# Down projection of a hybrid decoder block: a plain part of six chunks, then two-by-two Strassen products in 26 staggered visits

## Chip, cores and metric

One core of a Trainium2 chip runs the whole kernel in one launch. The metric is device microseconds from the first to the last instruction of the execution; less is better. All tensors are float32. TensorE (PE) multiplies in a reduced float32 form, so each product of two float32 matrices is made of three: high part by high part, high by low, low by high, where `hi` is the operand rounded by ScalarE (ACT) and `lo` the remainder taken by VectorE (DVE).

## The reference, cut to what matters

```python
x = x + merged @ w_o                                   # x: 512 tokens x 2048
h = rmsnorm(x, g_ffn)
u = causal_dwconv(h @ w_up, ffn_conv_w, ffn_conv_b)    # 3 taps, 2 x 5632 channels
ug, uv = split(u, 2)
x = x + (silu(ug) * uv) @ w_down                       # 5632 -> 2048: the down projection
h = rmsnorm(x, g_ple)
x = x + sigmoid(h @ w_ple_gate) * (p @ w_ple_proj)
out = rmsnorm(x, g_final)
```

Ahead of these lines stands the mixer: attention and a convolution branch, merged by gates.

## The kernel before

Activations lie transposed, 128 channels on the partitions and 512 tokens in a row; such a tile (`A()`, one of 75 slots of the pool `slots`) is the moving operand. The weight is the stationary operand, 128x128 per matmul.

`build` makes a list of groups, and `run` goes through their chunks in order. For each chunk it issues the loads of the next six chunks at most (`loads`, on SP's queue, `wraw` has 7 buffers), cuts the weights two or three chunks ahead into `whi` and `wlo` (`prep`, `cut`, L272 on ACT and L273 on DVE, four buffers each), issues the matmuls, evicts, and calls `pump`, which steps each background generator (`add_bg`). A scheduler then orders each engine's instructions; each engine works through its own list in order.

Three kinds of work follow one another behind the mixer:

- **Up projection**, 44 `Pair` groups, one per 128 hidden channels of each half. Each is a two-by-two Strassen product: seven products (`ORDER`), each of 8 weight blocks. A product's weight is one of seven sums of four weight quarters; two of the sums are begun in HBM during the mixer (`sums`, L933: SP copies one quarter, POOL's DMA queue adds another), the others are made by adding a quarter to `wraw` by a POOL DMA after the cut (L310). `pair_step` issues per block one matmul of 512 columns (hi weight by the operand's hi and lo halves) and one of 256 (lo weight by hi). The hidden tiles go to HBM (`hid`).
- **Down projection**, `Group`s over w_down: the 44 chunks of 128 hidden channels are split into `PARTS` of 12, 12, 12 and 8; each part fetches its hidden tiles from HBM and splits them (`fetch`, `split`), and goes through all 16 output tiles in four groups of four. Per chunk and output tile there are three matmuls of 512 columns (`products`, L417), so 44 x 16 x 3 = 2112. After each group `ev_down` (L960) adds the four PSUM tiles to the residual `x1`, which stands in SBUF.
- **Gate**, four groups over w_ple_gate, whose operand `h2` is `x1` split with the norm's weight (`split_x1`, `begin_gate`), while the norm's statistics (`stats("rb3")`, L185) run beside the first group. The last group is done twice, for tokens 0 to 255 and 256 to 511 (`TOK_A`, `again`), so its matmuls have 256 columns.

Of the kernel before, what the change touches and what calls it, by code (L numbers as in the profile page):

```python
# [1 line left out]

# [15 lines left out]
P = 128  # L18
# [41 lines left out]
class Group:  # L60


    def __init__(self, w, rhs, evict, tok=False, before=None, ns=ALL, keep=None):
        self.ns = ns
        self.w, self.rhs, self.evict, self.tok, self.before = w, rhs, evict, tok, before
        self.n = w.shape[0]
        self.nm = w.shape[3] // P
        self.keep = keep


class Pair:
# [9 lines left out]
    def __init__(self, src, rhs, evict, before=None, beside=()):  # L81
        self.src, self.rhs, self.evict, self.before, self.beside = src, rhs, evict, before, iter(beside)
        self.kh = src[1].shape[1]
        self.raw, self.cut, self.ps, self.c = {}, {}, {}, {}


class Kernel:
# [18 lines left out]
    def X(self):  # L106
        return self.aux.tile([P, S], F32, tag="x", name="x")

# [8 lines left out]

    def move(self, out, in_):

        self.nc.gpsimd.dma_start(out=out, in_=in_)  # L120
# [135 lines left out]
    def run(self, groups):  # L256
        nc = self.nc
        chunks = []
        for n, g in enumerate(groups):
# [3 lines left out]
            if not isinstance(groups[n - 1], Pair):  # L263
                chunks.append((g, 5))
            after = groups[n + 1] if isinstance(groups[n + 1], Pair) else None
# [9 lines left out]
        def dma(i, kks=(slice(0, 2),)):  # L275
            if i < len(chunks):
                g, c = chunks[i]
                if isinstance(g, Pair):
# [19 lines left out]
        def prep(i, kks=(slice(0, 2),)):  # L298
# [3 lines left out]
            if isinstance(g, Pair):  # L302
                hi = self.whi.tile([P, g.kh, P], F32R, tag="w", name="whi")
                lo = self.wlo.tile([P, g.kh, P], F32R, tag="w", name="wlo")
                raw = g.raw[{6: 5, 3: 5}.get(c, c)]
                cut(hi, lo, raw)
                g.cut[c] = hi, lo

# [17 lines left out]

        loadx = self.start(dma, prep)
        begun.update(range(3))
        cuts = 1
        for i, (g, c) in enumerate(chunks):  # L330
# [8 lines left out]
            if g.before and c == (5 if isinstance(g, Pair) else 0):  # L339
                g.before()  # L340
            if isinstance(g, Pair):
                self.pair_step(g, c)
                for _ in range(2):
                    next(g.beside, None)
                self.pump()
                continue
# [20 lines left out]
            if c == g.n - 1:  # L367
                g.evict(g.ps)
            self.pump()
# [12 lines left out]
    def pair_step(self, g, c):  # L382
# [21 lines left out]
        if p == 4:  # L404
            g.evict(g.c[1], g.c[6], g.c[4], g.c[5])

# [237 lines left out]
    def build(self):  # L644
# [224 lines left out]
        def fold(c, eng):  # L869
            eng.tensor_tensor(c[:, LEFT], c[:, LEFT], c[:, RIGHT], op=ALU.add)  # L870

# [33 lines left out]
        F0 = [sum(PARTS[:i]) for i in range(len(PARTS))]  # L905
        hs = {}

        def fetch(pi):
            raw = {}
            for f in range(F0[pi], F0[pi] + PARTS[pi] + 2):  # L910
                if f < F0[pi] + PARTS[pi]:
                    raw[f] = self.A()
                    self.move(out=raw[f], in_=hid[f])
                if f - 2 >= F0[pi]:
                    hs[f - 2] = self.split(raw.pop(f - 2))
                yield


        srcs = []
        for j in range(KF):  # L920
            w = t["w_up"][j]
            s1, s3 = (self.dram.tile([P, KD // 2 + 1, P], F32, tag=f"s{n}_{j}", name=f"s{n}_{j}")[:, :KD // 2] for n in (1, 3))
            srcs.append({1: w[0], 2: w[1], 4: w[3], 5: s1, 7: s3})

# [11 lines left out]
        builders = {0: fetch(0)}  # L936
        for j in range(KF):
            groups.append(Pair(srcs[j], lambda p, k: T2[p][k], ev_up(j), before=first_up if j == 0 else None,
                               beside=builders[0] if j == KF - 1 else ()))

        def ready(pi, mg):
            def f():
                if mg == 0:
                    if pi == 0:
                        self.finish_chains()
                    for _ in builders[pi]:
                        pass
                if pi == 0:
                    for m in range(4 * mg, 4 * mg + 4):
                        self.x1[m] = self.A()  # L950
                        self.load(out=self.x1[m], in_=x1d[m])
                if mg == 1 and pi + 1 < len(PARTS):
                    builders[pi + 1] = self.add_bg(fetch(pi + 1))
            return f

        def ev_down(mg):
            def f(ps):
                for m in range(4):
                    z = self.x1[4 * mg + m]
                    nc.vector.tensor_tensor(z, ps[m], z, op=ALU.add)  # L960
            return f

        for pi, n in enumerate(PARTS):
            for mg in range(4):
                groups.append(Group(t["w_down"][mg][F0[pi] // 2:(F0[pi] + n) // 2], lambda k, pi=pi: hs[F0[pi] + k],
                                    ev_down(mg), before=ready(pi, mg)))


        h2, pj = {}, {}

        def split_x1():
            for k in range(KD):
                h2[k] = self.split(self.x1[k], self.col(C_GPLE + k))
                self.nacc = self.square_add(self.x1[k], self.nacc)
                if k % 2:
                    yield
            yield from stats("rb3")()

        def begin_gate():
            self.g_split = self.add_bg(split_x1())  # L980
            next(self.g_split)
            next(self.g_split)

        def load_pj(mg):
            def f():
                if mg == 0:
                    begin_gate()
# [51 lines left out]
        for mg in range(4):  # L1039
            groups.append(Group(t["w_gate"][mg], lambda k: h2[k], ev_gate2(4 * mg, TOK_A if mg == 3 else ALL),  # L1040
# [72 lines left out]
```

## Time and profile before

| | us |
|---|---|
| three runs: median (lowest to highest) | 2762.07 (2758.61 to 2774.99) |
| the profiled execution | 2775.36 |
| its span in the trace | 2773.6 |
| PE busy in it | 2749.3 |
| DVE busy, ACT busy | 1738.3, 1149.1 |

The profiled execution lies 13.3 us above the median of the three runs. Busy time of PE is a modelled time: matmuls are pipelined, and a matmul of 512 columns is listed with 387 ns where the next one starts after some 227 ns. How fast PE goes is therefore read from counts in a stretch of time, and where it waits from its idle time.

### The profile page before, as it was taken

How to read it: one execution, taken by the hardware profiler on the slowest of the kernel's cores; microseconds unless marked ns; L12 is line 12 of the kernel's file. 1: busy time of each engine (PE TensorE's matmuls, PEld its weight loads, DVE VectorE, ACT ScalarE, POOL GpSimd, SP SyncE). 2: the span in 40 equal slices, each digit the busy share in tenths (PEclk: the TensorE clock that was granted, in tenths of full speed). 3: DMA queues.
4: the chain of work that ended last, by engine and by line, in shares of the span. 5: the costliest groups of instructions: out<-in, count | busy, mean ns of one | idle time of the engine just before them, and what ended most of it. 6: DMA issues, size and time to landing. Idle time of an engine off the chain costs nothing.

```text
span 2773.6 us, 34953 instructions
## 1 busy us (share of the span) xinstructions
PE 2749.3 (99%) x13528; PEld 2316.6 (84%) x13528; DVE 1738.3 (63%) x2554; ACT 1149.1 (41%) x1647; POOL 231.3 (8%) x320
## 2 busy tenths in 40 slices
PE   9999999999999999999999999999999999999997
PEld 7888888888888888888888888888888888888787
DVE  5465588658745454478787878787876433335436
ACT  5354452222123333356555555555554322113333
POOL 0010010000000000021111111111111000000000
PEclk9999999999999999999999999999999999999999
DMA  8574756767666674467777777777777433223322
GB/s 278 162 227 134 231 153 182 197 197 194 191 192 186 194 226 146 148 189 199 202 198 202 198 201 198 202 198 201 199 208 277 145 113 103 99 94 112 99 95 95
DMA packets 145303, 489.85 MB, mean 177 GB/s; under 512 B 17136, under 2 KB 21232, under 8 KB 145136
## 3 DMA queue, kind: packets, MB, share of 16 engines
q1 hardware_dynamic: 110048, 363.86, 38.7%
q0 software_dynamic: 34944, 123.75, 22.2%
q8 instruction: 106, 1.74, 0.2%
q14 instruction: 61, 0.50, 0.1%
q10 hardware_dynamic: 144, 0.01, 0.0%
HBM read 457.14 MB, written 116.39 MB: 207 GB/s over the span
## 4 chain that ended last, share of the span: by engine, by line
PE 97%; DVE 1%; issue 1%; ACT 0%; DMA 0%; POOL 0%; POOLq 0%; DVEq 0%; ACTq 0%
PE m L417 65%; PE m L393 20%; PE m L394 10%; PE x L553 1%; PE x L526 0%; PE x L527 0%; PE x L544 0%; DVE wlo L273 0%; DMA a<-hid 0%; DVE o L1033 0%; DVE a L165 0%; PE x L185 0%; DMA gm<-g_mix 0%; PE x L569 0%; POOL sm L217 0%
## 5 line engine op out<-in xcount | busy, mean ns | idle before, releaser
L417 PE MATMUL m<-a,whi 128*128 128x512 f32 (+1 forms) x5056 | 1542.5, 387 | 2.7 <-DVE a L1018 1.4
L273 DVE TENSOR_TENSOR wlo<-wraw,whi 128x1024 fp32r<-128x1024 f32 (+1 forms) x637 | 777.7, 1222 | 784.9 <-ACT whi L272 755.9
L272 ACT ACTIVATE whi<-wraw 128x1024 fp32r<-128x1024 f32 (+1 forms) x637 | 673.1, 1058 | 1360.4 <-PE m L417 899.6
L417 PEld LDWEIGHTS m<-a,whi 128*128 128x128 f32 x5056 | 942.8, 188 | 193.8 <-DVE a L1018 1.7
L417 PE MATMUL m<-a,wlo 128*128 128x512 f32 (+1 forms) x2528 | 976.1, 387 | 0.0
L393 PE MATMUL m<-a,whi 128*128 128x512 f32 x2464 | 871.1, 399 | 3.0 <-ACT a L397 2.0
L394 PE MATMUL m<-a,wlo 128*128 128x256 f32 x2464 | 692.0, 281 | 0.0
L393 PEld LDWEIGHTS m<-a,whi 128*128 128x128 f32 x2464 | 463.0, 188 | 119.3 <-ACT a L397 2.7
L417 PEld LDWEIGHTS m<-a,wlo 128*128 128x128 f32 x2528 | 474.4, 188 | 96.3 <-DVE wlo L273 0.3
L394 PEld LDWEIGHTS m<-a,wlo 128*128 128x128 f32 x2464 | 465.4, 189 | 0.2
L610 DVE SCALAR_TENSOR_TENSOR a<-a,par 128x485 f32<-128x485 f32 (+19 forms) x240 | 172.4, 733 | 6.1 <-ACT a L607 1.6
L933 POOL DMA_DIRECT2D s<-w_up x88 | 72.4, 826 | 827.8 <-DMA s<-w_up 827.8
L890 DVE SCALAR_TENSOR_TENSOR a<-a,par 128x511 f32<-128x511 f32 (+1 forms) x176 | 131.4, 747 | 1.9 <-ACT a L888 0.3
L310 POOL DMA_DIRECT2D wraw<-w_up x88 | 75.1, 854 | 343.2 <-DVE a L883 247.2
L397 ACT ACTIVATE a<-m 128x512 f32<-128x512 f32 x176 | 101.8, 578 | 0.0
L888 ACT ACTIVATE a<-a,par 128x512 f32<-128x512 f32 x88 | 71.1, 808 | 38.7 <-DVE a L885 38.7
L417 PE MATMUL m<-whi,a 128*128 128x512 f32 x256 | 81.7, 394 | 0.4 <-ACT whi L272 0.4
L150 ACT ACTIVATE a<-a 128x512 fp32r<-128x512 f32 x88 | 53.6, 624 | 58.1 <-DVE a L228 23.0
L151 DVE TENSOR_TENSOR a<-a 128x512 fp32r<-128x512 f32 x88 | 59.8, 688 | 17.3 <-ACT a L150 16.8
L217 POOL TENSOR_TENSOR sm<-sm,mhalf 128x4 f32<-128x4 f32 (+1 forms) x14 | 15.7, 1123 | 547.9 <-DVE sm L216 547.9
L120 POOL DMA_DIRECT2D hid<-a x44 | 25.4, 577 | 429.8 <-DVE a L895 429.8
L885 DVE TENSOR_TENSOR a<-a 128x512 f32<-128x512 f32 x88 | 60.2, 684 | 0.2
(136 smaller groups left out, 1348.0 us busy)
## 6 DMA issues: line engine op xcount, KB each, us to landing
wraw<-w_in SPq DMA_DIRECT2D x143, 512.0 KB, 4.2
wraw<-w_up SPq DMA_DIRECT2D x132, 512.0 KB, 3.7
s<-w_up SPq DMA_DIRECT2D x88, 512.0 KB, 5.9
s<-w_up POOLq DMA_DIRECT2D x88, 512.0 KB, 6.9
wraw<-s SPq DMA_DIRECT2D x88, 512.0 KB, 4.6
wraw<-w_up POOLq DMA_DIRECT2D x88, 512.0 KB, 5.5
wraw<-w_down SPq DMA_DIRECT2D x88, 512.0 KB, 3.5
wraw<-w_o SPq DMA_DIRECT2D x32, 512.0 KB, 3.6
```

The source lines that it names most:

```text
L272: nc.scalar.activation(hi, w, AF.Copy)
L273: nc.vector.tensor_tensor(lo, w, hi.bitcast(F32), op=ALU.subtract)
L310: nc.gpsimd.dma_start(out=raw, in_=g.src[{5: 1, 6: 2}[c]], accum_op=ALU.add)
L393: nc.tensor.matmul(ps, lhsT=hi[:, k], rhs=t, start=new and k == 0, stop=False, skip_group_check=True)
L394: nc.tensor.matmul(ps[:, LEFT], lhsT=lo[:, k], rhs=t[:, LEFT], start=False, stop=k == g.kh - 1, skip_group_check=True)
L397: nc.scalar.activation(x, ps, AF.Copy)
L417: nc.tensor.matmul(out, lhsT=l, rhs=r, start=first and n == 0, stop=last and n == 2)
L610: nc.vector.scalar_tensor_tensor(y[:, s:], u[:, :S - s], self.col(w + k), y[:, s:], op0=ALU.mult, op1=ALU.add)
L885: nc.vector.tensor_tensor(u, u, rb, op=ALU.mult)
L888: nc.scalar.activation(y, u, AF.Identity, scale=self.col(w + 2), bias=self.col(C_FB + ch))
L890: nc.vector.scalar_tensor_tensor(y[:, s:], u[:, :S - s], self.col(w + 2 - s), y[:, s:], op0=ALU.mult, op1=ALU.add)
L933: nc.gpsimd.dma_start(out=src[n], in_=w[h], accum_op=ALU.add)
```

## The change

The 5632 hidden channels are split: the first `F0` = 6 chunks stay plain, the other 38 make `KP` = 19 pairs. For these the down projection is a two-by-two Strassen product: two output tiles (`o` and its partner, 8 such pairs of tiles), two halves of the hidden channels of a pair, two halves of the tokens (`LEFT`, `RIGHT`, 256 each).

- `feed` fetches two hidden tiles of a pair and makes seven operand tiles of them (`operands`, as in the up projection: 4 sums and 7 hi/lo cuts of 256 columns). They are kept in `T3`, and as 19 x 7 don't fit into 75 slots, the outputs are visited in four rounds, staggered by one pair each: `VISITS` lists output, first and last pair.
- A visit with `kh` pairs has seven steps (`NARROW`). `visit_step` issues for each pair three matmuls of 256 columns into half a PSUM bank. The weight sums: one ("s") is made in HBM by `sums` behind those of the up projection (L993), two are added by DVE (L327, L329), one by a POOL DMA into `wraw` after the cut for product 6 (L333).
- Partial results, of the plain part too, are added to the residual in HBM by POOL DMAs (`ev_plain`, L1046, and L1077). At an output's last visit `x1` is loaded and summed on DVE (L1066), split into `h2`, and squared for the norm's statistics.
- The gate takes its operand in the order in which the outputs end (`GATE_K`).

```diff
-PARTS = [12, 12, 12, 8]
+F0 = 6
+KP = (KF - F0) // 2
+ENDS = [[2, 3, 4, 5, 6, 7, 8, 8], list(range(9, 17)), [min(n, KP) for n in range(17, 25)], [KP] * 2]
+NARROW = [1, 5, 6, 2, 7, 3, 4]
...
             if isinstance(g, Pair):
                 hi = self.whi.tile([P, g.kh, P], F32R, tag="w", name="whi")
                 lo = self.wlo.tile([P, g.kh, P], F32R, tag="w", name="wlo")
+                if not g.wide:
+                    a = g.raw
+                    if c == 6:
+                        nc.vector.tensor_tensor(a["s"], a["s"], a[0], op=ALU.add)
+                    elif c == 7:
+                        nc.vector.tensor_tensor(a[2], a[2], a[0], op=ALU.add)
+                    cut(hi, lo, a[{1: 0, 2: 1, 7: 2, 4: 3}.get(c, "s")])
+                    g.cut[c] = hi, lo
+                    if c == 6:
+                        nc.gpsimd.dma_start(out=a["s"], in_=g.src[1], accum_op=ALU.add)
+                    return
...
+    def visit_step(self, g, c):
...
+        for k in range(g.kh):
+            t = g.rhs(p, k)
+            for n, (w, x) in enumerate(((hi, LEFT), (hi, RIGHT), (lo, LEFT))):
+                nc.tensor.matmul(ps, lhsT=w[:, k], rhs=t[:, x], start=new and k == n == 0, stop=k == g.kh - 1 and n == 2,
+                                 skip_group_check=True)
...
         def sums():
...
+            for o in range(KD // 2):
+                for ks in (slice(0, KP // 2), slice(KP // 2, KP)):
+                    self.load(out=ds[o][:, ks], in_=t["w_down"][o, 2][:, ks])
+                    yield
+                    yield
+                    nc.gpsimd.dma_start(out=ds[o][:, ks], in_=t["w_down"][o, 3][:, ks], accum_op=ALU.add)
+                    yield
...
-        def ev_down(mg):
-            def f(ps):
-                for m in range(4):
-                    z = self.x1[4 * mg + m]
-                    nc.vector.tensor_tensor(z, ps[m], z, op=ALU.add)
-            return f
...
+            def chain(zs):
+                for m, z in zip(ms, zs):
+                    x = self.x1[m]
+                    nc.vector.tensor_tensor(x, z, x, op=ALU.add)
+                    h2[m] = self.split(x, self.col(C_GPLE + m))
+                    yield
+                    self.nacc3 = self.square_add(x, self.nacc3)
+                    yield
+            def evict(*zs):
+                if end:
+                    self.chain(chain(zs))
+                else:
+                    for m, z in zip(ms, zs):
+                        nc.gpsimd.dma_start(out=x1d[m], in_=z, accum_op=ALU.add)
...
+        for mg in range(4):
+            groups.append(Group(t["w_down0"][mg], lambda k: hs[k], ev_plain(mg), before=ready(mg), beside=islice(feeder, 9), rate=3))
+            made[0] += 9
+            if mg:
+                groups.append(visit(n))
+                n += 1
+        groups += [visit(k) for k in range(n, len(VISITS))]
```

Two places show how the change moves instructions. The first is POOL's list at the first pairs of the up projection. `wraw<-w_up` are the additions that complete a weight sum of the up projection, `pjd` and `hid` are stores of results. Before:

```order
L120 DMA pjd14_9639<-a_9637 128x512
L310 DMA wraw_9437<-w_up 128x1024
L120 DMA pjd15_9656<-a_9654 128x512
L310 DMA wraw_9588<-w_up 128x1024
L217 TENSOR_TENSOR sm_9775<-sm_9774,mhalf_235 128x4
L310 DMA wraw_9588<-w_up 128x1024
L310 DMA wraw_9815<-w_up 128x1024
L120 DMA hid0_9959<-a_9892 128x512
```

And now, where `d4` to `d6` are the sums of the down weights in HBM:

```order
L993 DMA d4_173<-w_down 128x1280
L120 DMA pjd15_9679<-a_9677 128x512
L340 DMA wraw_9459<-w_up 128x1024
L340 DMA wraw_9611<-w_up 128x1024
L993 DMA d5_174<-w_down 128x1152
L227 TENSOR_TENSOR sm_9802<-sm_9801,mhalf_243 128x4
L993 DMA d5_174<-w_down 128x1280
L340 DMA wraw_9611<-w_up 128x1024
L340 DMA wraw_9842<-w_up 128x1024
L993 DMA d6_175<-w_down 128x1152
```

Seven of the sixteen additions of `sums` for the down weights stand among the first additions of the up projection; the other nine stand ahead, in the mixer.

The second place is DVE's list where the down projection ends and the gate begins. `wlo<-wraw` 128x1024 are cuts of gate weights, `m` is PSUM. Before, with the last evictions of the down projection at L960:

```order
L273 TENSOR_TENSOR wlo_20909<-wraw_20876,whi_20908 128x1024
L273 TENSOR_TENSOR wlo_20943<-wraw_20906,whi_20942 128x1024
L960 TENSOR_TENSOR a_18606<-m_20818,a_18606 128x512
L960 TENSOR_TENSOR a_18608<-m_20819,a_18608 128x512
L960 TENSOR_TENSOR a_18610<-m_20820,a_18610 128x512
```

And now, where the rows of 128 columns are cuts of the last visit (`kh` = 1), L463 and L466 its evictions and `wlo_23695` the first cut of a gate weight:

```order
L287 TENSOR_TENSOR wlo_23663<-wraw_23602,whi_23662 128x128
L287 TENSOR_TENSOR wlo_23676<-wraw_23564,whi_23675 128x128
L287 TENSOR_TENSOR wlo_23686<-wraw_23636,whi_23685 128x128
L466 SCALAR_TENSOR_TENSOR a_23671<-m_23646,a_23671 128x256
L463 TENSOR_TENSOR a_23650<-m_23667,a_23650 128x256
L1066 TENSOR_TENSOR a_23642<-a_23650,a_23642 128x512
L1066 TENSOR_TENSOR a_23644<-a_23671,a_23644 128x512
L287 TENSOR_TENSOR wlo_23695<-wraw_23660,whi_23694 128x1024
```

The gate's first two cuts stood ahead of the last evictions, and the first of them now stands behind the last visit's evictions and its two additions to the residual.

## Rows read from the trace of the kernel before

**Rows 1.** The page: span, and each engine's busy time, share, instructions

```profile
span 2773.6 us, 34953 instructions
...
PE 2749.3 (99%) x13528; PEld 2316.6 (84%) x13528; DVE 1738.3 (63%) x2554; ACT 1149.1 (41%) x1647; POOL 231.3 (8%) x320
```

**Rows 2.** The page's chain that ended last, by engine and by line

```profile
PE 97%; DVE 1%; issue 1%; ACT 0%; DMA 0%; POOL 0%; POOLq 0%; DVEq 0%; ACTq 0%
PE m L417 65%; PE m L393 20%; PE m L394 10%; PE x L553 1%; PE x L526 0%; PE x L527 0%; PE x L544 0%; DVE wlo L273 0%; DMA a<-hid 0%; DVE o L1033 0%; DVE a L165 0%; PE x L185 0%; DMA gm<-g_mix 0%; PE x L569 0%; POOL sm L217 0%
```

**Rows 3.** Busy time by stretch: up, down, gate's half-width part, joins

```profile
core 0: us, PE busy (x) PEld busy (x) DVE busy (x) ACT busy (x) POOL busy (x), PEclk, DMA share, GB/s
1300.00:1400.00 100.00, 100.00 (x568) 86.69 (x567) 81.43 (x106) 56.92 (x71) 11.39 (x15) 1.00 0.76 201
1245.00:2070.00 825.00, 825.00 (x4671) 715.40 (x4670) 675.66 (x878) 478.12 (x590) 96.89 (x128) 1.00 0.76 200
2100.00:2200.00 100.00, 100.00 (x443) 82.77 (x442) 50.75 (x64) 35.42 (x46) 11.24 (x21) 1.00 0.56 197
2711.50:2739.00 27.50, 27.50 (x230) 27.42 (x229) 17.29 (x32) 13.55 (x26) 0.00 (x0) 1.00 0.19 74
1220.00:1240.00 20.00, 19.91 (x112) 16.92 (x111) 14.70 (x29) 10.66 (x16) 4.89 (x7) 1.00 0.90 272
2120.00:2140.00 20.00, 20.00 (x90) 16.57 (x89) 11.35 (x16) 8.90 (x14) 3.76 (x7) 1.00 0.97 367
2615.00:2640.00 25.00, 22.60 (x98) 17.90 (x97) 16.49 (x32) 13.41 (x19) 1.03 (x1) 1.00 0.20 60
```

**Rows 4.** Instruction groups by line: busy us, mean ns of one, idle before

```profile
L273 DVE TENSOR_TENSOR wlo<-wraw,whi 128x1024 fp32r<-128x1024 f32 (+1 forms) x637 | 777.7, 1222 | 784.9 <-ACT whi L272 755.9 <-PE x L553 21.0 <-PE x L544 3.0
L272 ACT ACTIVATE whi<-wraw 128x1024 fp32r<-128x1024 f32 (+1 forms) x637 | 673.1, 1058 | 1360.4 <-PE m L417 899.6 <-PE m L393 312.1 <-issue 69.3
L397 ACT ACTIVATE a<-m 128x512 f32<-128x512 f32 x176 | 101.8, 578 | 0.0
L960 DVE TENSOR_TENSOR a<-m,a 128x512 f32<-128x512 f32 x64 | 43.3, 691 | 18.2 <-PE m L417 18.2
L165 DVE TENSOR_TENSOR a<-a 128x256 fp32r<-128x256 f32 x48 | 18.0, 418 | 0.1
L164 ACT ACTIVATE a<-a 128x256 fp32r<-128x256 f32 x48 | 17.0, 405 | 4.7 <-DVE a L171 4.5 <-DVE a L174 0.2
L154 DVE SCALAR_TENSOR_TENSOR a<-a,par 128x512 fp32r<-128x512 f32 x16 | 11.9, 746 | 0.0
```

**Rows 5.** PE's timeline, its two waits at the start of the up projection

```profile
1208.46 0.73 PE L417 MATMUL m<-a,whi 128*128 128x512 f32 x2 [1.27 <-DVE a L849]
...
1241.10 0.50 PE L393 MATMUL m<-a,whi 128*128 128x512 f32 x1 [0.91 <-DVE a L401]
```

**Rows 6.** DMA issues: KB each, median us from issue to landing

```profile
s<-w_up SPq DMA_DIRECT2D x88, 512.0 KB, 5.9
s<-w_up POOLq DMA_DIRECT2D x88, 512.0 KB, 6.9
...
wraw<-w_up POOLq DMA_DIRECT2D x88, 512.0 KB, 5.5
...
x1d<-a POOLq DMA_DIRECT2D x16, 256.0 KB, 2.7
```

**Rows 7.** Line L310, the additions into `wraw`: issue ns, spread of landings

```profile
L310 POOL DMA_DIRECT2D wraw<-w_up x88: 845/855/902, 1215.0 to 2075.4; - x88
...
DMA to landing us min/median/max: 5.2/5.5/9.7
```

**Rows 8.** Tile `s`, the weight sums made in HBM: spread of their landings, both queues

```profile
DMA to landing us min/median/max: 3.5/5.5/16.6
```

More of the change, by code (lines that the diff above doesn't have):

```diff
@@ L1 @@
 from contextlib import ExitStack
+from itertools import islice
 import numpy as np
@@ L262, in run @@
                 continue
-            if not isinstance(groups[n - 1], Pair):
+            if not g.wide:
+                chunks += [(g, p) for p in NARROW]
+                continue
+            near = [isinstance(x, Pair) and x.wide for x in (groups[n - 1], groups[n + 1])]
+            if not near[0]:
                 chunks.append((g, 5))
-            after = groups[n + 1] if isinstance(groups[n + 1], Pair) else None
+            after = groups[n + 1] if near[1] else None
             chunks += [(after if p == 5 else g, p) for p in ORDER if p != 5 or after]
@@ L277, in dma @@
                 g, c = chunks[i]
+                if isinstance(g, Pair) and not g.wide:
+                    for h in {1: (0,), 5: ("s",), 2: (1,), 7: (2,), 4: (3,)}.get(c, ()):
+                        g.raw[h] = self.wraw.tile([P, g.kh, P], F32, tag="w", name="wraw")
+                        self.load(out=g.raw[h], in_=g.src[h])
+                    return
                 if isinstance(g, Pair):
@@ L368, in run @@
                 g.evict(g.ps)
+            for _ in range(g.rate):
+                next(g.beside, None)
             self.pump()
@@ L902, in ev_up @@
             return f
[L905 to L916, printed above, removed]
         srcs = []
@@ new lines, in ev_plain, with f, visit, before @@
+        def ev_plain(mg):
+            def f(ps):
+                for m, x in enumerate(ps):
+                    z = self.A()
+                    nc.scalar.activation(z, x, AF.Copy)
+                    nc.gpsimd.dma_start(out=x1d[4 * mg + m], in_=z, accum_op=ALU.add)
+            return f
+        h2, pj = {}, {}
+        self.nacc3 = None
+        def visit(n):
+            o, i, e = VISITS[n]
+            ms = 2 * o, 2 * o + 1
+            end = e == KP
+            def before():
+                if end:
+                    for m in ms:
@@ new lines, in evict @@
+            def evict(*zs):
+                if end:
+                    self.chain(chain(zs))
+                else:
+                    for m, z in zip(ms, zs):
+                        nc.gpsimd.dma_start(out=x1d[m], in_=z, accum_op=ALU.add)
+            more = max(0, 7 * VISITS[n + 1][2] - made[0]) if n + 1 < len(VISITS) else 0
+            made[0] += more
+            src = {h: t["w_down"][o, h][:, i:e] for h in range(4)}
+            src["s"] = ds[o][:, i:e]
+            return Pair(src, lambda p, k: T3[p][i + k], evict, before,
+                        islice(feeder, more), wide=False)
```

124 lines of the change are left out of this document (82 added, 42 removed).

## The prediction

> **What bounds the kernel now.** I read the page first. PE is busy for 2749.3 of 2773.6 us, DVE for 63% and ACT for 41% [rows 1]. The chain that ended last then shows whether this is a bound or an average: 97% of it is PE, by its matmul lines [rows 2]. So the time is the sum of PE's stretches, and what helps is fewer PE microseconds, as long as nobody keeps PE waiting. The third view is the busy time by stretch, for PE's true pace [rows 3]. In the down projection 443 matmuls of 512 columns take 100 us, 0.2257 us each. In the gate's half-width part 230 matmuls of 256 columns take 27.5 us, 0.1196 each; that is the form which the visits issue three times per pair of chunks (hi, hi, lo). The clock is 1.00 in both. The fourth view is who has room: in the up projection, work of the same kind as the visits, DVE is busy for 675.66 of 825 us (82%), the DMA share is 0.76, and PE still shows no idle time [rows 3].
>
> **The change, part by part.**
>
> *Matmuls.* Removed: 2112 of 512 columns at 0.2257 = 476.7 us. Added: the plain part, 6 x 16 x 3 = 288 at 0.2257 = 65.0 us, and the visits. The lengths of all visits sum to 8 x 19 = 152, so they issue 152 x 7 x 3 = 3192 matmuls of 256 columns, at 0.1196 = 381.8 us. Sum: -29.9 us. Strassen saves one eighth of 38/44 of the columns, some 11% or 51 us, of which two fifths are lost since two matmuls of 256 columns take 0.2392 us against 0.2257.
>
> The loader of weights shows why: in the 256-column stretch PEld is busy for 27.42 of 27.50 us, in the 512-column one for 82.77 of 100 [rows 3]. The Trainium skill, "TensorE: Matmul & The Clock Gate", section "LDWEIGHTS (loading the stationary operand)", says that a load costs by the weight's columns alone, 128 of them some 107 ns, however few columns then stream. It speaks against narrower matmuls, and the full loader agrees; its 107 ns as the pace would give (an estimate) 340.5 us for the visits and -71 in all, but the trace has 119.6 ns for the same thing, and I use that.
>
> Could the pace be worse in the visits than in that quiet stretch (DVE 63% busy, DMA share 0.19)? The up projection gives a bound: 568 matmuls, half of each width, take 100 us, 0.3521 a pair against 0.2257 + 0.1196 = 0.3453, that is 2% more [rows 3]. On 381.8 us that would be 7.6. I take 0, since the stretch is of the very same form, and keep 0 to 8.
>
> *DVE and ACT in the visits.* From the rows for 1024 and 256 columns [rows 4] a cut takes DVE about 0.15 + 0.134 kh us and ACT 0.19 + 0.109 kh (kh pairs of 128 columns). A visit with 7 pairs lasts 7 x 21 x 0.1196 = 17.6 us on PE. DVE has seven cuts and two sums of 1.09, eleven operand steps at 0.418 and three evictions at 0.42: 15.7 us, 89%. Up to 82% is shown to be hidden; 89% is not. ACT has some 60%. I take 1 us for all visits of 5 pairs or more, between 0 (the up projection) and 6.
>
> *Weight sums in the visits.* DVE's cut of product 6 releases a POOL addition, which product 3 needs, three steps later. At 7 pairs, from the eviction of the product 3 before: eviction 0.42, cut 1.09, addition 5.5 [rows 6], cut on ACT 0.95 and DVE 1.09, matmuls 2.5: 11.6 us in a visit of 17.6. Hidden.
>
> *The short last visits.* The last five visits have 5, 4, 3, 2 and 1 pairs. The same loop, with a sum for product 6 on DVE and the residual addition (0.69, [rows 4]) ahead of that cut, does not shrink as PE's part does. A small addition into `wraw` is not in the trace. I bound it by the plain store of 256 KB, 2.7 us, and the addition of 512 KB, 5.5 us [rows 6], and take the middle, 4.1. Loops: kh 3: 0.42 + 0.55 + 0.55 + 0.69 + 4.1 + 0.51 + 0.55 + 1.08 = 8.45 against a visit of 7.53; kh 2: 7.6 against 5.02; kh 1: 6.7 against 2.51; kh 4: 9.3 against 10.0. PE waits 0.9 + 2.6 + 4.2 = 7.7 us. Bounds: 4.0 with 2.7 us, 12.6 with 5.5.
>
> The Trainium skill, "DMA: Bandwidth & Descriptors", section "Anatomy of one DMA — SWDGE (gpsimd) path", gives about 2 us plus bytes by 436 GB/s for a DMA of this queue. For 128 KB that is (an estimate) 2.3 us instead of 4.1, and the waits would be about 3 us; its 3.2 us for 512 KB is well under the 5.5 of [rows 6], so I don't lean on it.
>
> *Entry of the gate.* Its first cut now waits for the last visit's whole eviction. From PE's last matmul: eviction on ACT 0.41, hi cut 1.06, lo cut 1.22, less the two hi matmuls (0.45) that PE can do meanwhile: 2.2 us of new wait, between 1 and 4. Tail in all: 10 us, 5 to 16.
>
> *The norm's statistics.* Now squares are summed visit by visit and finished before the gate starts; before, they were made beside its first group, and PE idled for 25.0 - 22.6 = 2.4 us there [rows 3]. That goes: -2.4 (0 if the tail delays them as long).
>
> *Sums in HBM.* Sixteen copies and additions of 576 to 640 KB. Nine fall into the mixer's end, where POOL and DMA have room. Seven additions stand among the first of the up projection. There DMA is at 0.90 and 272 GB/s in [1220, 1240], and PE has its two waits of 1.27 and 0.91 us already [rows 3, 5]. POOL works in order: it holds for each copy (median 5.9 us, up to 16.6 for these tiles [rows 6, 8], issued two steps ahead, a step being 8 x 0.3521 = 2.8 us), and behind it wait the additions that products 3 and 6 of the pair need. Slack is three steps, 8.5 us, less 5.5, plus the cuts' lead. I take 4 us, between 0 and 11 (one landing of 16.6 instead of 5.9).
>
> *The rest.* Residual additions in HBM (52 stores, at most some 0.9 us of POOL each by [rows 7]) lie beside PE and are waited for a round later. The fetches are earlier than needed. The join of plain groups and the first short visits costs cuts that come just in time: 1.5 us, 0 to 4.
>
> *Sum.* -29.9 - 2.4 + 1 + 10 + 4 + 1.5 = -15.8 us. Against the profiled execution's 2775.4 this is 2759.6; that execution lies 13.3 above the median of the runs, so I forecast 2762.1 - 15.8 = 2746.3, 0.6% less. A measurement of this kernel can tell about 1%, 27.6 us, from no change.
>
> **The rivals.**
>
> *No stalls.* If small additions land in 2.7 us or less and the sums in HBM disturb nothing, some 5 us of waits are left: -29.9 - 2.4 + 5 = -27 and down to -31: 2731 to 2735, at the edge of 1%. For it: the up projection runs with full DVE and DMA and no idle PE. Against: PE's two waits at its start [rows 5], and visits of 1 to 3 pairs are a regime that no row shows. Chance 0.16.
>
> *A slower pace of the 256-column matmuls.* Two per cent (above) gives back 7.6: 2754. Chance 0.14.
>
> *The sums in HBM hit the up projection's start.* 11 us instead of 4, from POOL's order: 2753; with a bad tail as well 2760. Chance 0.12.
>
> *Slower: the addition for product 3 sets the pace of every visit.* Place: POOL's queue, visits of 7 and 8 pairs, of which there are 15. It decides from 5.5 + (17.6 - 11.6) = 11.5 us of landing; each microsecond beyond costs 15. A landing of 15.5 us gives +60, net +44: 2806; one of 14 gives 2784. For it: landings of 9.7 us [rows 7] and 16.6 [rows 8] have happened, with DMA near its ceiling. Against: a visit moves six weight loads of 459 KB and four tiles of 262 KB in 17.6 us, 216 GB/s beside 200 in the up projection, and DMA gave 367 at a share of 0.97 [rows 3]. Chance 0.09.
>
> **How the numbers follow.** Forecast 0.49, with its own range 2735 to 2764. No stalls 0.16, of which 0.13 lies over 1%; with 0.01 of the forecast's low end that makes faster 0.14. The slower rival has 0.09, of which 0.07 lies beyond 1%. All else is within it: 0.79. The ends of the terms, -29.9 - 2.4 + 5 = -27 and -29.9 + 8 + 6 + 16 + 11 + 4 = +15, are seldom met together; I widen the low end for the no-stall case and stop the high one at 2775.
>
> **What would show it.** Right: in the visits, stretches of PE without idle time at 0.119 to 0.122 us a matmul; PE's idle time in the last three visits and at the gate's first matmul, some 10 us, put down to ACT's and DVE's cuts and behind them to the addition into `wraw`; no 2.4 us at the norm's statistics; DVE at 85 to 90% in the visits; PE's waits at the start of the up projection grown from 2 to some 6 us. Wrong: a pace of 0.125 or more; waits of PE at product 3 of each visit; ACT waiting for `wraw` by the POOL queue for more than 2 us per visit; tail waits under 4 or over 18 us.

## The result, and the profile after

Four runs of the changed kernel have a median of 2845.74 us (2840.13 to 2847.01), four of the kernel before beside them 2768.53: a ratio of 1.028, 95% interval 1.024 to 1.032. The change is 2.8% slower where 0.6% faster was forecast, and lies above the 2775 us at which the forecast's range stops. The profiled execution has a span of 2843.9 us, 70.3 above that of before; 34953 instructions became 38877.

Where the 70 us came from shows by stretches. First the start of the up projection and all of the visits, after; the columns are those of [rows 3]:

```profile
1215.00:1320.00 105.00, 91.92 (x486) 78.72 (x485) 72.52 (x108) 51.48 (x73) 20.15 (x27) 0.92 0.95 261
...
1450.00:1550.00 100.00, 100.00 (x568) 86.67 (x567) 81.92 (x107) 57.60 (x71) 11.50 (x15) 1.00 0.78 200
...
2145.00:2643.00 498.00, 442.08 (x3331) 428.52 (x3330) 330.23 (x538) 236.72 (x446) 82.80 (x104) 0.95 0.70 180
```

And the same first stretch before:

```profile
1215.00:1320.00 105.00, 104.00 (x581) 89.50 (x580) 86.85 (x128) 63.06 (x88) 16.68 (x23) 1.00 0.78 211
```

*Start of the up projection.* 486 matmuls instead of 581; 95 at 0.176 us (half of the pair's 0.3521) are 16.7 us. Some 12 of these are idle time of PE (13.1 us instead of 1.0), the rest is the granted clock, 0.92 in this stretch. Behind it both run at one pace (568 in 100 us).

*The visits.* From the first to the last matmul of the visits, 498.5 us, stand 3192 matmuls of 256 columns and 144 of the plain part (its third and fourth group): 381.8 + 32.5 = 414 us at the paces of [rows 3]. So 84 us are lost. PE's idle time there, from the groups by line, is 56 us. The other 28 are the pace behind the waits: the granted clock is 0.95 on average (0.83 to 0.92 in ten of the 25 stretches of 20 us from 2145 on), and by the starts of the matmuls in the trace 213 follow their predecessor after 0.220 us without idle time, the others after 0.120, as at the lower of the clock's two levels (1.2 instead of 2.4 GHz):

```profile
L455 PE MATMUL m<-a,whi 128*128 128x256 f32 x2128 | 404.4, 292 | 55.5 <-ACT a L460 40.7 <-ACT whi L286 8.1 <-DVE a L466 6.5
L455 PE MATMUL m<-a,wlo 128*128 128x256 f32 x1064 | 308.1, 290 | 0.5 <-DVE wlo L287 0.5
```

With what the prediction had right, 16.7 + 84 - 29.9 (columns) - 2.4 (norm's statistics) is 68 of the 70 us; 1.4 more are PE's wait at the gate's first matmul.

Who was waited for in the visits, in the views of waits of ACT and of DVE, stretch 2120 to 2680 (us in total, times, longest):

```profile
ACT whi L286 <- DMA wraw<-w_down: 86.2, 20, 7.8
...
DVE wraw L329 <- DMA wraw<-w_down: 53.2, 11, 6.8
DVE wraw L329 <- issue: 26.1, 5, 5.9
```

The addition for product 3, line L333, landed after:

```profile
DMA to landing us min/median/max: 3.3/8.0/9.4
```

One visit of 7 pairs shows how this reaches PE. ACT's timeline, with gaps and what ended them in brackets:

```profile
2424.35 0.95 ACT L286 ACTIVATE whi<-wraw 128x896 fp32r<-128x896 f32 x1 [1.03 <-PE m L455]
2425.21 0.36 ACT L460 ACTIVATE a<-m 128x256 f32<-128x256 f32 x1
2425.47 0.41 ACT L174 ACTIVATE a<-a 128x256 fp32r<-128x256 f32 x1
2432.53 0.95 ACT L286 ACTIVATE whi<-wraw 128x896 fp32r<-128x896 f32 x1 [6.66 <-DMA wraw<-w_down]
2433.39 0.36 ACT L460 ACTIVATE a<-m 128x256 f32<-128x256 f32 x1
2433.66 0.41 ACT L174 ACTIVATE a<-a 128x256 fp32r<-128x256 f32 x1
2433.96 0.94 ACT L286 ACTIVATE whi<-wraw 128x896 fp32r<-128x896 f32 x1
2434.80 0.37 ACT L460 ACTIVATE a<-m 128x256 f32<-128x256 f32 x1
```

DVE, POOL and PE at the same time:

```profile
2426.34 0.42 DVE L175 TENSOR_TENSOR a<-a 128x256 fp32r<-128x256 f32 x1
2432.68 1.09 DVE L329 TENSOR_TENSOR wraw<-wraw 128x896 f32<-128x896 f32 x1 [5.92 <-issue]
2433.69 1.08 DVE L287 TENSOR_TENSOR wlo<-wraw,whi 128x896 fp32r<-128x896 f32 x1
...
2423.64 0.89 POOL L333 DMA_DIRECT2D wraw<-w_down  x1 [0.74 <-DVE wlo L287]
...
2435.22 0.80 PE L455 MATMUL m<-a,whi 128*128 128x256 f32 x2 [3.30 <-ACT a L460]
...
2436.03 0.63 PE L455 MATMUL m<-a,whi 128*128 128x256 f32 x2
...
2436.67 0.63 PE L455 MATMUL m<-a,whi 128*128 128x256 f32 x2
```

POOL issues the addition at 2423.6; it has landed when ACT's cut for product 3 starts at 2432.5. Behind this cut, in ACT's list, stands the eviction of product 6 (2434.80), and only then may PE write the same PSUM bank for product 7 (2435.22). Three matmuls then take 0.64 us (2436.03 to 2436.67), where three take 0.36 at the pace of [rows 3]. DVE stands too, until 2432.7, at the sum for product 7 of the *next* visit, whose load has come at the same time. The next L333 is issued 22 us after this one, and the visit's matmuls need 17.6. The lists show both orders, here for another visit (ACT, then DVE; `wraw_21962` is the sum for products 6 and 3, `m_22149` the bank of products 1, 6, 7 and 4, `wraw_22323` a tile of the next visit):

```
L286 ACTIVATE whi_22181<-wraw_22073 128x1024
L460 ACTIVATE a_22174<-m_22149 128x256
L174 ACTIVATE a_22176<-a_21749 128x256
L286 ACTIVATE whi_22218<-wraw_21962 128x1024
L460 ACTIVATE a_22211<-m_22186 128x256
L174 ACTIVATE a_22213<-a_21994 128x256
L286 ACTIVATE whi_22256<-wraw_22143 128x1024
L460 ACTIVATE a_22174<-m_22149 128x256

L287 TENSOR_TENSOR wlo_22182<-wraw_22073,whi_22181 128x1024
L175 TENSOR_TENSOR a_22176<-a_21749,a_22176 128x256
L329 TENSOR_TENSOR wraw_22323<-wraw_22323,wraw_22179 128x1024
L287 TENSOR_TENSOR wlo_22219<-wraw_21962,whi_22218 128x1024
```

At the start of the up projection it is POOL that stands, as foreseen (waits in 1195 to 1330). But what PE waits for there is again an eviction on ACT, behind cuts that wait for additions which POOL issued late (ACT's same wait was 8.0 us before):

```profile
POOL d L993 <- DMA d<-w_down: 40.6, 6, 13.9
...
ACT whi L286 <- DMA wraw<-w_up: 29.5, 5, 12.4
...
PE m L429 <- ACT a L433: 13.1, 3, 7.0
```

Runs of the kernel before fall into two groups, some 2760 and 2775 us, as do those of several kernels below, and profiles show either some 579 or some 568 matmuls in 100 us of the up projection, at a granted clock of 1.00 in both, so stretches are compared below besides totals.

### The profile page after: what moved, and what is told of

It is laid out like the page before. It is cut to its first block, busy times and chain, and to the rows that moved or that the text cites. A ratio compares the mean times of both kernels' runs of the same rounds, so it can differ in the third digit from the quotient of the medians.

```text
span 2843.9 us, 38877 instructions
## 1 busy us (share of the span) xinstructions
PE 2752.7 (97%) x14896; PEld 2382.3 (84%) x14896; DVE 1896.6 (67%) x2913; ACT 1269.4 (45%) x1968; POOL 316.9 (11%) x414
## 3 DMA queue, kind: packets, MB, share of 16 engines
q1 hardware_dynamic: 120128, 383.78, 40.6%
## 4 chain that ended last, share of the span: by engine, by line
PE 79%; issue 13%; DMA 3%; POOL 2%; DVE 1%; ACT 1%; POOLq 0%; SPq 0%; DVEq 0%; ACTq 0%
PE m L481 47%; PE m L429 19%; PE m L430 9%; DMA wraw<-w_up 1%; PE m L455 1%; DMA d<-w_down 1%; DMA wraw<-w_down 1%; POOL a L120 1%; PE x L617 1%; PE x L590 0%; POOL x1d L1077 0%; POOL wraw L333 0%; DVE wlo L287 0%; PE x L591 0%; ACT whi L286 0%
## 5 line engine op out<-in xcount | busy, mean ns | idle before, releaser
L286 ACT ACTIVATE whi<-wraw 128x1024 fp32r<-128x1024 f32 (+7 forms) x743 | 741.1, 1000 | 1311.7 <-PE m L481 592.2
L287 DVE TENSOR_TENSOR wlo<-wraw,whi 128x1024 fp32r<-128x1024 f32 (+7 forms) x743 | 853.4, 1151 | 626.6 <-ACT whi L286 597.6
L481 PE MATMUL m<-a,whi 128*128 128x512 f32 (+1 forms) x3840 | 1169.8, 387 | 2.7 <-ACT whi L286 1.4
L481 PEld LDWEIGHTS m<-a,whi 128*128 128x128 f32 x3840 | 715.6, 188 | 146.4 <-ACT whi L286 1.7
L481 PE MATMUL m<-a,wlo 128*128 128x512 f32 (+1 forms) x1920 | 739.7, 386 | 0.0
L430 PE MATMUL m<-a,wlo 128*128 128x256 f32 x2464 | 694.0, 282 | 0.0
L429 PEld LDWEIGHTS m<-a,whi 128*128 128x128 f32 x2464 | 465.4, 189 | 132.6 <-ACT a L433 16.5
L430 PEld LDWEIGHTS m<-a,wlo 128*128 128x128 f32 x2464 | 467.8, 190 | 0.2
L455 PE MATMUL m<-a,whi 128*128 128x256 f32 x2128 | 404.4, 292 | 55.5 <-ACT a L460 40.7
L481 PEld LDWEIGHTS m<-a,wlo 128*128 128x128 f32 x1920 | 360.7, 188 | 72.9 <-DVE wlo L287 0.3
L455 PEld LDWEIGHTS m<-a,whi 128*128 128x128 f32 x2128 | 345.2, 199 | 63.0 <-ACT a L460 44.4
L455 PE MATMUL m<-a,wlo 128*128 128x256 f32 x1064 | 308.1, 290 | 0.5 <-DVE wlo L287 0.5
L455 PEld LDWEIGHTS m<-a,wlo 128*128 128x128 f32 x1064 | 211.6, 199 | 1.2 <-DVE wlo L287 1.2
L329 DVE TENSOR_TENSOR wraw<-wraw 128x896 f32<-128x896 f32 (+7 forms) x26 | 24.3, 935 | 81.4 <-DMA wraw<-w_down 55.4
```

Source lines behind the costliest of these rows:

```text
L286: nc.scalar.activation(hi, w, AF.Copy)
L287: nc.vector.tensor_tensor(lo, w, hi.bitcast(F32), op=ALU.subtract)
L429: nc.tensor.matmul(ps, lhsT=hi[:, k], rhs=t, start=new and k == 0, stop=False, skip_group_check=True)
L430: nc.tensor.matmul(ps[:, LEFT], lhsT=lo[:, k], rhs=t[:, LEFT], start=False, stop=k == g.kh - 1, skip_group_check=True)
L455: nc.tensor.matmul(ps, lhsT=w[:, k], rhs=t[:, x], start=new and k == n == 0, stop=k == g.kh - 1 and n == 2, skip_group_check=True)
L481: nc.tensor.matmul(out, lhsT=l, rhs=r, start=first and n == 0, stop=last and n == 2)
```

## The experiments

"Visits" is the time from the first to the last matmul of line L455 (whatever its number there), "start" the count of matmuls in 1215 to 1320 us, "pace" the count in 1450 to 1550, all from the profiled run, so these three have no interval. Where nothing in the order of the visits was changed (after, e1, e8, e18) they took 498.5 to 502.9 us. In the ten runs that leave the sums in HBM at the start, the count there lies 95 to 143 below that of an undisturbed start at the same pace, 17 to 25 us. Ratios are to runs of the kernel before on the same chip.

| run | median us | ratio, 95% interval | visits us | start | pace |
|---|---|---|---|---|---|
| before | 2768.5 | | | 581 | 568 |
| after | 2845.7 | 1.024 to 1.032 | 498.5 | 486 | 568 |
| e1_no_down_sums | 2818.6 | 1.016 to 1.025 | 502.9 | 590 | 579 |
| e2_no_p3_add | 2800.0 | 1.007 to 1.017 | 459.7 | 449 | 579 |
| e3_no_resid_acc | 2807.8 | 1.012 to 1.018 | 468.8 | 467 | 579 |
| e4_none | 2745.8 | 0.991 to 0.996 | 429.3 | 585 | 579 |
| e5_pin_p7_sum | 2807.9 | 1.014 to 1.019 | 460.7 | 455 | 567 |
| e6_p3_last | 2867.7 | 1.035 to 1.041 | 519.0 | 476 | 568 |
| e7_p3_pool_add | 2803.2 | 1.011 to 1.018 | 458.2 | 478 | 579 |
| e8_spread_sums | 2845.8 | 1.027 to 1.032 | 499.2 | 570 | 568 |
| e9_pin_pool_add | 2779.0 | 1.001 to 1.006 | 434.6 | 477 | 569 |
| e10_no_hbm_sums | 2791.4 | 1.005 to 1.011 | 466.1 | 586 | 579 |
| e11_raws8 | 2842.7 | 1.022 to 1.032 | 484.9 | 462 | 568 |
| e13_no_hbm_raws8 | 2771.1 | 1.000 to 1.006 | 446.9 | 592 | 579 |
| e14_behind | 2839.7 | 1.022 to 1.032 | 497.7 | 473 | 578 |
| e15_behind_pin | 2792.6 | 1.004 to 1.012 | 447.2 | 479 | 579 |
| e16_behind_pin_early | 2777.9 | 1.002 to 1.007 | 453.3 | 580 | 567 |
| e17_early_pool | 2747.4 | 0.992 to 0.996 | 433.7 | 591 | 579 |
| e18_early_only | 2822.6 | 1.017 to 1.026 | 502.3 | 576 | 567 |
| e19_early_pool_behind | 2746.5 | 0.993 to 0.998 | 431.8 | 592 | 579 |

**Leaving transfers out**, one at a time and all three.

```diff
-            for o in range(KD // 2):                         # e1, e4: the loop of L993
-            src["s"] = ds[o][:, i:e]
+            src["s"] = t["w_down"][o, 2][:, i:e]
-                        nc.gpsimd.dma_start(out=a["s"], in_=g.src[1], accum_op=ALU.add)    # e2, e4
-                        nc.gpsimd.dma_start(out=x1d[m], in_=z, accum_op=ALU.add)           # e3, e4
```

> The sixteen sums of the down weights in HBM are left out (the visits load the bare quarter for product 5, so one weight sum is missing in the output). Theory A, these copies and additions keep the first up pairs waiting: the up projection ends 20 to 25 us earlier, PE's idle time between 1215 and 1320 us falls from 13 to about 2 us, total about 2820. Rival, the stretch is full anyway and the waits only change their releaser: less than 6 us, total 2838 to 2846. The visits (2145 to 2643 in the changed kernel, 498 us) keep their length either way.

> POOL's addition into wraw for product 3 is left out, product 3 then multiplies by product 6's sum (one weight quarter is missing in product 3). Theory B, this addition, landing after 8 to 9 us, paces the visits: the stretch of 498 us shrinks to about 430 (its matmuls alone are 419), total about 2775 to 2785. Rival C, the 7 wraw buffers and the late loads pace them (DVE's sum for product 7 stands in order ahead of the next cuts): the visits stay above 470 us, total 2815 to 2840. The up projection's start keeps its loss.

> The visits' partial results aren't added to the residual in HBM (only an output's last visit counts, so partial sums are missing). Theory D, these transfers of 256 KB, issued by POOL just before the addition for product 3, make that addition late: it lands in 5 to 6 us instead of 8 to 9, the visits shrink by 30 us or more, total 2790 to 2815. Rival B, the addition is late by itself (loads and fetches beside it): less than 10 us, total 2835 to 2846.

> All three are left out together: no sums of the down weights in HBM, no addition for product 3, no residual additions of the visits (three parts of the sum are missing in the output). If these transfers are the whole loss, the visits run at 0.12 us a matmul, about 425 us for the stretch that took 498, the up projection starts without the loss, and the total is 2735 to 2755. Rival, the matmuls of 256 columns or DVE and ACT at 89 and 60 per cent hold the pace back by themselves: the visits stay above 450 us, total 2770 to 2790.

e1: the start has its matmuls back (590), the visits don't shrink: theory A. e2: 39 us of the visits go, between the two forecasts (its 419 us of matmuls counted too many of the plain part; they are 414). DVE's early sum still waits (45.9 us for its load). e3: 30 us go, and the addition lands sooner, as its line shows against 8.0 above:

```profile
DMA to landing us min/median/max: 3.2/5.8/7.8
```

e4: visits of 429.3 us, and the total of 2745.8 is what had been forecast. So these transfers are most of the loss, 69 of the 84 us in the visits and the start's, and the pace of 256 columns and the load of DVE and ACT can be no more than the 15 us left. The gains of e2 and e3, 39 and 30 us, add up to e4's, but neither says by which link the transfers reach PE.

**The link: in whose list?**

```diff
+                        self.tc.keep_in_program_order(      # e5: of the sum of L329
                         nc.vector.tensor_tensor(a[2], a[2], a[0], op=ALU.add)
-NARROW = [1, 5, 6, 2, 7, 3, 4]                              # e6, with the evict moved to product 3
+NARROW = [1, 5, 6, 2, 7, 4, 3]
-                        nc.gpsimd.dma_start(out=a["s"], in_=g.src[1], accum_op=ALU.add)
+                    elif c == 3:                            # e7
+                        nc.gpsimd.tensor_tensor(a["s"], a["s"], a[1], op=ALU.add)
-RAWS = 7
+RAWS = 8                                                    # e11, and SLOTS 73
```

> DVE's sum for product 7 is pinned behind what stands before it in the program, so that it no longer stands in DVE's list a visit early, just ahead of the cut for product 3; nothing is left out. Theory H, that early sum, waiting for a late load, is what stops DVE: the visits shrink by 30 us or more, total 2795 to 2815. Rival L, the loop (DVE's cut for product 6, addition by POOL of about 9 us, cut for product 3, and then all the rest of the visit on DVE, 10 to 12 us, in order): the cut for product 3 waits at the same place by itself, and at most the 1.09 us of the sum move into the wait, 0 to 15 us in all, total 2830 to 2846.

> Order of a visit's products 1, 5, 6, 2, 7, 4, 3 instead of 1, 5, 6, 2, 7, 3, 4: product 3 comes last, one step later behind product 6; the output is the same. Theory L (loop of addition and the rest of DVE's list): the cut for product 4 and the operand work behind it, 1.1 to 3 us, move from behind the addition into its shadow, so each of some 20 visits gets that much shorter: visits 440 to 475 us instead of 498, total 2785 to 2825. Rival H (the early sum for product 7 on DVE, which still stands ahead of both cuts): less than 8 us, total 2836 to 2846.

> The sum for product 3 is made by POOL itself from the quarter that is already loaded for product 2, instead of by an addition through POOL's DMA queue; nothing is left out. Theory L: the loop loses its 9 us of landing and gets some 2 to 4 us of POOL's own work; visits 425 to 460 us instead of 498, total 2770 to 2800. Rival, the loads, later for one buffer that is held longer, and the residual additions pace the visits anyway, as without the addition: visits 460 us, total 2800 to 2815; or POOL's work slows DVE's, then no gain over the run without the addition and up to 20 us more.

> Only the number of buffers changes: wraw 8 instead of 7, two slots fewer for the tiles in exchange; nothing is left out. Theory C, the early sum for product 7 waits because the loads it needs come late for want of a buffer: DVE's waits at that sum (79 us) halve, the visits shrink by 20 us or more, total 2800 to 2826. Rival, the loads are late because of the transfers beside them, not for want of a buffer: less than 8 us, total 2837 to 2850.

e5, with every transfer in place, takes 38 us off, as theory H had it and not L. e6 was to help by L and cost 20 us in the visits, as neither forecast had it. Products 7 and 4 share a PSUM bank and now follow each other directly, so PE waits for DVE's eviction between them:

```profile
PE m L455 <- DVE a L468: 30.3, 15, 2.9
```

so e6 says nothing against or for a longer distance as such. e7 takes 40 us off; POOL's own addition takes 2.4 us (median) where the DMA landed after 8.0. e11 limits H: with the eighth buffer DVE hardly waits at the early sum (53.2 + 26.1 us before)

```profile
DVE wraw L329 <- DMA wraw<-w_down: 11.6, 12, 4.6
```

and the visits gain 13.6 us only, between its two forecasts. The pin of e5 had also let ACT's list come out another way (the evictions of products 1 and 5 ahead of the cuts for 7 and 3), and PE's waits for ACT's eviction are 20.6 us there instead of 40.7; how the other 24 us split between that and DVE isn't settled.

**Two together, and ACT's list alone.** e14, e15 and e19 change two things in the visits: the place of product 3's cut on ACT, and cutting two steps ahead instead of three.

```diff
+            # e9: the edits of e5 and e7; e15: that of e5 with this
-            while cuts < min(i + (3 if isinstance(g, Pair) else 2), len(chunks) - 1):
+            while cuts < min(i + (3 if isinstance(g, Pair) and g.wide else 2), len(chunks) - 1):
+                    # e14, e15, e19: hi cut for product 3 ordered behind g.ev6, product 6's eviction
```

> Both edits that shortened the visits together: DVE's sum for product 7 pinned in its place, and product 3's sum made by POOL from the quarter loaded for product 2; the output is complete. If they relieve two different waits (the early sum that stops DVE, and the late addition), the gains add: visits 425 to 440 us instead of 498, total 2765 to 2785. If they relieve the same wait by two ways, the visits stay at 455 to 462 us, total 2795 to 2808.

> Only ACT's order changes: in a visit the high cut for product 3 is put behind product 6's eviction (weights are cut two steps ahead instead of three in the visits); transfers and sums are as in the changed kernel, nothing is left out. Theory M: PE can't begin product 7 since the bank's eviction of product 6 stands on ACT behind the cut for product 3, which waits for the addition. Then PE's waits for ACT's eviction fall from 41 to under 10 us, and the visits from 498 to 450 to 475 us, total 2795 to 2822. Rival L, DVE's list (addition, then the rest of the visit's work, in order) sets the visit's length: PE's waits only change their releaser, visits above 485 us, total 2832 or more.

> ACT's order as in the run before and DVE's sum for product 7 pinned in its place; the addition for product 3 stays a DMA of POOL's queue, nothing is left out. Theory M with H: both in-order lists no longer hold back near work for the late addition, which then lies hidden: visits 428 to 445 us instead of 498, total 2762 to 2790. Rival L, a late addition costs whatever the order, since DVE does most of a visit's work behind it: visits as with the pinned sum alone, 455 to 465 us, total 2798 to 2812.

e9: the gains nearly add up (38 and 40 apart, 64 together, of the 84 lost), within the forecast for two different waits; of PE's 56 us of idle time in the visits 10 are left:

```profile
L455 PE MATMUL m<-a,whi 128*128 128x256 f32 x2128 | 388.8, 285 | 8.3 <-ACT whi L286 6.2 <-ACT a L460 1.8 <-DVE a L466 0.2
```

e14: theory M fell, and the numbers are those of rival L. PE waits for the same eviction as long as before. Ahead of it on ACT now stand operand cuts (L174), and these wait for DVE's operand sums, which are queued behind the early sum:

```profile
PE m L458 <- ACT a L463: 40.6, 17, 5.0
...
ACT a L174 <- DVE a L181: 86.1, 14, 8.5
...
DVE wraw L332 <- DMA wraw<-w_down: 66.6, 14, 7.5
```

With the sum pinned the same order of ACT gives 447.2 us instead of 460.7 (e15), between its two forecasts and nearer to M with H, and PE's waits for ACT's eviction fall from 20.6 to 3.3 us. So both lists carry the stop, one into the other: freeing ACT alone gained nothing, freeing both 51 us with every transfer in place.

**The sums in HBM**: spread, gone, or done earlier.

```diff
-                    yield                                   # e8, twice: before and behind L993's addition
+                    yield from self.rest(8)
+        def down_sums():                                    # e16 to e19: a generator of its own
+            yield from self.rest(SUMS_FROM + 100)
+                        a["s"] = self.wraw.tile(...)        # e10, e13: no sums in HBM, on e9
+                        nc.gpsimd.tensor_tensor(a["s"], a[2], a[3], op=ALU.add)
```

> The sixteen sums of the down weights in HBM are spread over the up projection: eight steps between a copy and its addition, eight to the next copy, instead of one and none; nothing is left out. Theory A, what costs is seven of them one after the other among the first up pairs, with POOL's list held by each copy: the start of the up projection loses 3 us or less and nothing is lost later, total 2818 to 2828. Rival, the transfers cost the up projection their time wherever they stand, since its DMA share is 0.76 already: total 2835 to 2846.

> Only the sums of the down weights in HBM move: begun some 76 steps earlier, all done in the mixer; nothing is left out. By the counts of matmuls at the up projection's start (486 against 581 in 105 us) they cost 16.7 us there: the same stretch then shows 575 to 585 matmuls, the up projection ends that much earlier, total 2825 to 2832 at the slower of its two paces, 2809 to 2816 at the faster. The visits keep 495 to 505 us. Rival: the mixer's end pays for it, total 2838 to 2846.

> As the run before with pinned sum and POOL addition, and the sums of the down weights in HBM are gone too: POOL adds the quarters for products 7 and 4, which are loaded anyway, into a buffer of its own for product 5; the output is complete, and a visit loads four tiles instead of five. Theory A (sums in HBM among the first up pairs): 10 to 25 us less than that run, from the up projection's start; and if the transfers of a visit are what is left of its waits, 10 us more from the visits: total 2740 to 2765. Rival: two POOL additions of 2.4 us in a row and loads that have to come earlier make product 5 late, visits no shorter or longer, total 2765 to 2790.

> The run without sums in HBM, with pinned sum and POOL additions, and 8 wraw buffers instead of 7, two slots fewer; the output is complete. If buffers still hold the loads back there, 5 to 15 us less than with 7, total 2735 to 2755; if not, the same within 4 us, or more by waits of the operand tiles for slots.

e8: the start is nearly whole (570), but the loss comes later, in two stretches that hold 1134 matmuls each before:

```profile
1500.00:1700.00 200.00, 196.57 (x1107) 170.22 (x1106) 159.98 (x209) 112.03 (x139) 27.11 (x35) 0.99 0.84 222
1700.00:1900.00 200.00, 192.57 (x1076) 166.91 (x1075) 153.88 (x200) 107.73 (x133) 25.32 (x33) 0.98 0.82 212
...
POOL d L992 <- DMA d<-w_down: 75.4, 14, 8.6
```

so the rival was right that they cost their time wherever they stand in the up projection. POOL is held at each copy there too, but the DMA share is 0.84 and 0.82 as well, and no run separates the two. e18 moves them into the mixer, where the stretch 900 to 1200 keeps its 1325 matmuls: start 576, and at the same pace the profiled run lasts 2835.2 instead of 2845.6, 10 us less, with 4 more in the visits. So the sums cost some 14 us by this and 17 to 25 by the counts; e18's median mixes both paces. e10 and e13 do without sums in HBM, but their visits are longer than e9's, by 31 and 12 us. e10 came out just above the range of its rival; the eighth buffer of e13 takes 19 us off the visits, so loads waited for buffers there, and what the other 12 are isn't settled.

**Both causes taken away.**

> As the run before, and the sums of the down weights in HBM are begun some 76 steps earlier, beside those of the up projection, so that all sixteen are done in the mixer; nothing is left out. Theory A: the up projection's start loses 3 us or less, 10 to 25 us less than the run before and nothing more in the mixer. Rival: the mixer has no room for both (its DMA share is 0.7 there), PE waits there, no gain.

> The run with the pinned sum and POOL's own addition (visits 435 us, 2779), with all sums of the down weights done in the mixer; nothing is left out. Theory A: 10 to 25 us less, total 2752 to 2769, that is level with the kernel before or up to 0.4 per cent below it. Rival: the mixer pays, total 2772 or more.

> The run of 2747 us (sum for product 7 pinned, POOL's own addition for product 3, sums in HBM done in the mixer) with ACT's order changed as well: the cut for product 3 behind product 6's eviction, weights cut two steps ahead instead of three; nothing is left out. If ACT's order still holds PE back, the visits shrink from 434 to 425 to 430 us, total 2738 to 2744. If it mattered only for the late addition: within 3 us; or up to 10 us more, since cuts two steps ahead leave less room.

e16 is e15, e17 is e9, each with the sums done in the mixer; e19 is e17 with ACT's order. e17 does all the change was to do, with nothing left out: 2747.4 us, below its forecast and 0.6% (0.4 to 0.8) under the kernel before. Its visits from 2250 to 2500 us, and the same stretch before these edits:

```profile
2250.00:2500.00 250.00, 250.00 (x2085) 249.94 (x2084) 210.06 (x295) 133.40 (x234) 67.04 (x54) 1.00 0.61 174
2250.00:2500.00 250.00, 223.85 (x1741) 221.21 (x1739) 158.44 (x245) 109.98 (x195) 42.32 (x56) 0.94 0.70 179
```

No idle time in e17, 0.1199 us a matmul, with DVE busy for 84%. e16, with the addition left to the DMA queue, gets to 2777.9, short of that: its start is whole (580), but its visits are 6 us longer than e15's. In e19 ACT's order gives 1.9 us more in the visits: within the 3 us of the forecast's second case.

## Why the prediction was wrong

*The step that failed* is "Weight sums in the visits", which ended in "Hidden". It set a loop of 11.6 us against a visit of 17.6. Two things were off. The size: the addition took 5.5 us in it and 8.0 in the trace, with four transfers of 256 KB of POOL's queue and two weight loads of SP's beside it (without the residual's two: 5.8). That alone makes 14 us, still less than 17.6. By the Trainium skill, "DMA: Bandwidth & Descriptors", section "Anatomy of one DMA — SWDGE (gpsimd) path", 448 KB would take about 3.1 us (an estimate); the trace's 8.0 is far from it. What decided is the second: the loop held the chain's own instructions only. It went through two in-order lists, and I never asked what stands behind the blocked cut: on ACT the eviction that releases product 7's bank, one product earlier than product 3; on DVE the sum for the next visit, and behind it the cut, the operand sums and all else of the visit. The visit of 7 pairs became 21 to 22 us, and all visits lost 84. The lists that show it were fixed before the run; the prediction drew on POOL's and on the entry of the gate's alone.

*The slower rival* had the right place and sign, with a chance of 0.09, and a wrong point of decision: it asked for a landing of 11.5 us, by the same short loop, while 8.0 was enough. Its "against" (bytes per visit, 216 GB/s) compared means: the transfers of a visit start together (DMA share 0.81 to 1.09 from 2424 to 2432), while in 2420 to 2422 the share is 0.00.

*Sums in HBM at the first up pairs*: right mechanism (POOL holds for each copy, 40.6 us), mis-sized term: 4 us (0 to 11) against 16.7. The error is the same: the slack was counted up to the product that needs the addition, while PE stopped earlier, at an eviction that stands on ACT behind the waiting cut (13.1 us in three waits). Behind these waits the granted clock adds the rest (0.92 in that stretch).

*The clock after waits* had no term at all. In the visits it is most of the 28 us beside 56 of idle time.

*Right*: the columns saved and the 0.1196 us (0.1199 in e17); that DVE (84% in e17, 89 forecast) and ACT hide their cuts there; the tail: PE idle for 9.3 us from 2600 to 2643 and 1.4 at the gate's entry, and 8.9 and 7.7 us from one addition to the next in the last three visits, where loops of 8.45 and 7.6 had been worked out; the 2.4 us of the norm's statistics. Without the two stalls these terms come close to the time: e17 has 2747.4, forecast 2746. The closeness is in part luck: e17's visits take 19 us more than their columns, where 12.5 (1 + 10 + 1.5) were put down for them and the gate's entry, and its start costs nothing, where 4 were put down.

## What to carry to other kernels

A loop through several engines is as long as its chain plus whatever stands behind each blocked instruction in that engine's in-order list; read these lists at the place before calling a transfer hidden. Ask above all which eviction is queued behind a cut that waits for a DMA, since PE stops at the PSUM bank and not at the product that needs the data. A scheduler may put a ready-looking sum of the next round ahead of it; one pin was worth 38 us (it changed ACT's list too), and a sum made by an engine from tiles already loaded was worth as much as leaving it out.

## What was not expected of the hardware

- Transfers beside each other land later: the addition into `wraw` after 8.0 us, and after 5.8 without the residual's stores (e3). Those stores, 256 KB with addition, landed after 6.4 us (median of the 36 of the visits, 4.5 to 11.7), the plain stores of before after 2.7 [rows 6]; what of this is the addition and what the traffic beside it isn't shown.
- The up projection's pair of matmuls takes 0.352 or 0.345 us, in profiles of kernels whose code there is the same (568 or 579 in 100 us, granted clock 1.00, no idle time). Over 2464 pairs this is 16 us, about the distance of the two groups in which the times of one kernel fall. What chooses isn't shown. The slower pace that the prediction took for a bound of the visits was this.
- POOL's own addition in SBUF took 2.4 us (median of all 26 in e17, the widths mixed; the nine of 128x896 took 2.66 on average):

```profile
L329 POOL TENSOR_TENSOR wraw<-wraw x26: 736/2400/3457, 2113.2 to 2540.3; 128x896 f32<-128x896 f32 x9, 128x1024 f32<-128x1024 f32 x6, 128x256 f32<-128x256 f32 x2, 128x384 f32<-128x384 f32 x2
```
